# The recurrence's side work on GpSimd's queue, in four steps a group instead of three

## The chip, the cores and the metric

The kernel runs on one core of one Trainium2 chip. The metric is the device time of one execution in microseconds (us). The engines are PE (TensorE, matmuls), DVE (VectorE), ACT (ScalarE), POOL (GpSimd) and SP (SyncE); the last issues most DMAs. ACT and POOL can issue DMAs too; all of them move over the core's 16 DMA engines.

## The reference, cut to what matters

Two models run one after the other on 256 tokens of width 1024, with 256 context tokens beside them in the first. The first has two layers, each a token mixer followed by a mixture of 32 experts, of which each token uses two:

```python
def expert_block(args):               # xb: a block of gathered tokens, e: its expert
    xb, e = args
    hb = jax.nn.silu(xb @ w1[e]) * (xb @ w3[e])
    return hb @ w2[e]
...
y = ypad.reshape(-1, D)[dest] * weights[order][:, None]
return jnp.zeros_like(xt).at[tok].add(y)
```

The second model is a layer of dilated attention and then a diagonal complex recurrence:

```python
A = lax.complex(a_re, a_im);  dt = jnp.exp(log_dt)[:, None]
a_bar = jnp.exp(A * dt)
b_bar = ((a_bar - 1.0) / A)[..., None] * Bm          # Bm = b_re + i b_im
bu = jnp.einsum('bsgc,gpc->bsgp', uf, b_bar)
_, states = lax.associative_scan(combine, (a_elems, bu), axis=1)
y = jnp.einsum('bsgp,gcp->bsgc', states, Cm).real    # Cm = c_re + i c_im
```

The parameters of the recurrence (a, b, c, dt) do not depend on the tokens, so that tables of powers and products of them can be made long before the recurrence runs.

## The kernel before

`run()` calls the stages in order: setup, `phase_a`, `moe(0)`, `phase_b`, `moe(1)`, `phase_c` (attention), `phase_d` (recurrence). The change lies in `moe(1)`, the second mixture. Its 32 experts are worked through in ten groups, p = 0 to 9, by the list `PLAN[1]`: two experts in p = 0 and 1, three in p = 2 to 5, four in p = 6 to 9. The instructions of the groups stand in the order in which the code is written (`tc.manual_schedule()`), on every engine.

An expert's weights come as six DMAs of 1 MB on SP's queue (`w()`, L176), so a group has 12, 18 or 24 of them. They land in eleven slots of 1 MB, seven named `wt` and four named `wu`, that are used in turn: a load takes the slot of the load eleven before it, and waits until PE has read that one. The DMAs of SP and ACT share eight semaphores in turn, so that an SP load also waits until the DMA eight before it, whoever issued it, has landed.

A group runs so: `hidden()` multiplies the gathered tokens with w1 and w3 in four blocks, (h,m) = (0,0), (0,1), (1,0), (1,1); each block reads a sixth of the group's loads. Between the matmuls of the first two blocks the group before is scattered back, four times: PE makes `px` (L1322, L1323), DVE multiplies it with the gate into `yt` (L1325), POOL adds that to `x` (L1329). `px` has two buffers, so the third `px` waits for the first `yt`. Then come the gate product `sg` (ACT L1284, DVE L1285 and L1286), the gathering of the next group's tokens (PE L1233), transposes (L1292, L1259), and `result()`, which multiplies with w2 into `py` (PE L1304) and ends with the two `yl` on DVE (L1312). At the start of a group DVE also makes the one-hot matrices of the next one (L1214 to L1222).

The tables of the recurrence are made beside this by a generator, `ssm_side()`, whose `yield`s cut it into steps. `next(side, None)` runs one step where it stands: in `hidden()` after the blocks (0,0) and (0,1), and after `result()`, from p = 1 on. The steps are, by number: 1 the DMAs of parameters and raw tensors; 2 PE transposes of a (L1854) and powers on DVE; 3 `turned(0)`, 32 PE transposes of the raw b (L1846) and copies by ACT and DVE; 4 arithmetic on DVE; 5 `turned(1)`, the same transposes for c; 6 arithmetic; 7 nothing; 8 the power tables E and U (DVE); 9 `bb` and `EB` (DVE and POOL); 10 `Bg` (DVE and POOL); 11 sixteen PE transposes of `Bg` (L2031) and a store of 1 MB to the scratch `Sd`; 12 `Wd`; 13 four matmuls (L2047) and `KC` on DVE; 14 to 17 the same as 10 to 13 for the other half; 18 to 20 `CP` and the first powers (`turn`); 21 to 24 further powers (`unit`), then two stores of 1 MB. With three steps a group, p = 1 runs steps 1 to 3, p = 2 steps 4 to 6, and so on to p = 8.

Of the kernel before, what the change touches and what calls it, by code (L numbers as in the profile page):

```python
# [11 lines left out]
F32 = mybir.dt.float32  # L12
# [9 lines left out]
P = 128  # L22
# [96 lines left out]
class Model:  # L119
# [911 lines left out]
    def moe(self, l):  # L1031
        nc, A, tc, m = self.nc, self.A, self.tc, self.m
# [51 lines left out]
        def rest():  # L1084

            nonlocal side, G2
            m.c4.close()
            xl = c3.enter_context(tc.tile_pool(name=f"xl{l}", bufs=1, side="right"))
            G2 = G2 or gates(xl)
            if l == 1:  # L1090
                self.row_bc(A["final_g"], m.fg, nc.sync)
                side = self.ssm_side(xl, psum)

        fixed, by_count = PLAN[l]
# [171 lines left out]
        def hidden(ws, xT, between=iter(()), turn=True, ts=PAIR):  # L1266
            ph = [psum.tile([P, 512], F32, name=f"ph{m}") for m in range(2)]
            for h in range(2):
                for m in range(2):
                    for k in range(4 * h, 4 * h + 4):  # L1270
                        for j, r in slots(ts)[1]:
                            nc.tensor.matmul(ph[m][r, :], lhsT=xT[:, k, r], rhs=ws[m, j, h][:, k % 4, :],  # L1272
                                             start=(k == 0), stop=(k == NK - 1))
                        if k % 2 == 1:
                            next(between, None)
                    if h == 0 and turn:
                        next(side, None)
            for _ in between:
                pass

            sg = xe.tile([P, 512], F32, name="sg", tag="sg")
            sv = sg.rearrange("p (h k c) -> p h k c", h=2, k=2)
            pv = [v.rearrange("p (h c k) -> p h k c", h=2, k=2) for v in ph]
            nc.scalar.activation(sv, pv[0], AF.Sigmoid)  # L1284
            nc.vector.tensor_mul(sv, sv, pv[0])  # L1285
            nc.vector.tensor_mul(sv, sv, pv[1])  # L1286
            return sg
# [519 lines left out]
    def ssm_side(self, p, psum):  # L1807


        nc, A = self.nc, self.A  # L1810
        ident = self.ident
# [11 lines left out]
        ad = x2[0:64, 0:256].rearrange("p (i d q) -> p i d q", i=2, d=2)  # L1823
        for i, n in enumerate(("ssm_a_re_2", "ssm_a_im_2")):
            for d in range(2):
                nc.scalar.dma_start(ad[:, i, d, :], A[n][0])
        s = p.tile([P, 16, 64], F32, name="sv", tag="sc")
        dt = s[:, 14]
        a = A["ssm_log_dt_2"]
        nc.scalar.dma_start(dt, bass.AP(tensor=a.tensor, offset=a.offset, ap=[[0, P], [1, 64]]))  # L1830

        bb = p.tile([P, 2, 64, 16], F32, name="bb")
        cc = p.tile([P, 2, 64, 16], F32, name="cc")
        b12 = p.tile([P, 2, 64, 16], F32, name="b12", tag="big")
        raws = [self.w(A[n][0].rearrange("g q c -> g (q c)"), (1024,), rows=64) for n in ("ssm_b_re_2", "ssm_b_im_2")]
        raws += [self.w(A[n][0].rearrange("g c q -> g (c q)"), (1024,), rows=64) for n in ("ssm_c_re_2", "ssm_c_im_2")]

        def turned(half):
            for i in (2 * half, 2 * half + 1):
                dst = (b12 if i < 2 else cc)[:, i % 2]  # L1840
                rv = raws[i].rearrange("g (q c) -> g c q", c=16) if i < 2 else \
                    raws[i].rearrange("g (c q) -> g c q", c=16)
                for c8 in range(2):
                    pt = pst()
                    for c in range(8):
                        nc.tensor.transpose(pt[0:64, c * 64:(c + 1) * 64], rv[:, c8 * 8 + c, :], ident[:64, :64])  # L1846
                    for h in range(2):
                        self.copy(dst[64 * h:64 * h + 64, :, c8 * 8:c8 * 8 + 8],
                                  pt[0:64].rearrange("p (c g) -> p g c", c=8), "av"[h])

        yield
        pt = pst()
# [42 lines left out]
        er, th, n, r, r2, cr = (s[:, i] for i in range(6))  # L1895
# [79 lines left out]
        for h in range(2):  # L1975
            rows = slice(64 * h, 64 * h + 64)
# [14 lines left out]
            return xt().rearrange("p (g c) -> p g c", c=16)  # L1991

        yield

        for hf in range(2):
            fr, fi = (F[:, i, 32 * hf:32 * hf + 32] for i in range(2))
# [8 lines left out]
        stage = self.cx.rearrange("p b d -> p (b d)")  # L2005
# [5 lines left out]
            ts(EB[64:128, sel, :, i], E[64:128, 0:4, bot], sb_, None, op0=ALU.mult)  # L2011

        bbM = p.tile([P, 32, 16], F32, name="bbM")
        for hf in range(2):
            yield

            Bg = p.tile([P, 16, 4, 2, 16], F32, name="Bg", tag="big")
            for sidx in range(4):
                j = 3 - sidx
                xa = ga()  # L2020
                gt(xa, hv(bb[:, 0], hf), gb(EB[:, 0, j, 0, 32 * hf:32 * hf + 32]), op=ALU.mult)
                tt(xb, hv(bb[:, 1], hf), gb(EB[:, 0, j, 1, 32 * hf:32 * hf + 32]), op=ALU.mult)
                xs = [t.rearrange("p (a b) c -> p a b c", b=2) for t in (xa, xb)]
                tt(Bg[:, :, sidx], xs[0], xs[1], op=ALU.add)
                if j == 0:
                    gt(bbM, xa, xb, op=ALU.add)
            yield
            for q in range(4):
                pt = pst()
                for i in range(4):  # L2030
                    nc.tensor.transpose(pt[:, i * P:(i + 1) * P], Bg[:, 4 * q + i].rearrange("p s g c -> p (s g c)"),  # L2031
                                        ident)
                self.copy(stage[:, q * 512:(q + 1) * 512], pt)
            nc.scalar.dma_start(self.Sd[hf], stage)
            yield

            Wd = p.tile([P, 4, 32, 16], F32, name="Wd", tag="big")
            for j in range(4):
                xa = ga()
                gt(xa, hv(c1, hf), gb(EB[:, 1, j, 0, 32 * hf:32 * hf + 32]), op=ALU.mult)  # L2040
                tt(xb, hv(cim, hf), gb(EB[:, 1, j, 1, 32 * hf:32 * hf + 32]), op=ALU.mult)
                tt(Wd[:, j], xa, xb, op=ALU.add)
            yield
            KC = p.tile([P, 4, 64], F32, name="KC")
            for ch in range(4):
                pt = pst()
                nc.tensor.matmul(pt, lhsT=bbM[:, 8 * ch:8 * ch + 8, :].rearrange("p g c -> p (g c)"),  # L2047
                                 rhs=Wd[:, :, 8 * ch:8 * ch + 8, :], start=True, stop=True)
                kt = xt().rearrange("p (d n) -> p d n", d=4)
                tt(kt, pt.rearrange("p (d n) -> p d n", d=4), self.cc("bmask")[:, None, :].to_broadcast([P, 4, P]),  # L2050
                   op=ALU.mult)
                nc.vector.tensor_reduce(KC[:, ch].rearrange("p (d c) -> p d c", d=4), kt.rearrange("p d (g c) -> p d c g", c=16), axis=AX.X,
                                        op=ALU.add)
            nc.scalar.dma_start(self.Sm[:, 1280 + 256 * hf:1536 + 256 * hf], KC.rearrange("p k n -> p (k n)"))
        yield

        CP = p.tile([P, 2, 32, 16], F32, name="CP", tag="sc")
        for h in range(2):
            rows = slice(64 * h, 64 * h + 64)
            nc.gpsimd.tensor_copy(CP[rows], cc[rows].rearrange("p i (a g) c -> p i a g c", g=2)[:, :, :, h, :])  # L2060
        for c0, t in ((0, CP.rearrange("p i a c -> p (i a c)")), (1024, E1.rearrange("p t i a -> p (t i a)")),
                      (1792, U1[:, 2])):
            nc.scalar.dma_start(self.Sm[:, c0:c0 + t.shape[1]], t)


        T = [t.rearrange("p i g c -> p (i g c)").rearrange("p (a k) -> p a k", k=64) for t in (bb, cc)]
# [22 lines left out]
        def unit(c):  # L2089
            v = [t[:, :, c:c + 16] for t in T]  # L2090
            a_, b_ = two()
            gt(a_, v[0], v[0], op=ALU.mult)
            tt(b_, v[1], v[1], op=ALU.mult)
            tt(b_, a_, b_, op=ALU.add)
            ts(b_, b_, -0.5, 1.5, op0=ALU.mult, op1=ALU.add)
            for t in v:
                tt(t, t, b_, op=ALU.mult)
# [11 lines left out]
        for c in range(0, 64, 16):  # L2109
            yield  # L2110
            unit(c)
        for n, t in enumerate(T):
            nc.scalar.dma_start(self.Sd[2 + n], t.rearrange("p a k -> p (a k)"))

    def phase_d(self):
        nc, A, tc = self.nc, self.A, self.tc
# [70 lines left out]
        E1 = SM[:, 1024:1280].rearrange("p (t i a) -> p i a t", i=2, a=32)  # L2187
        KC = SM[:, 1280:1792].rearrange("p (k d c) -> p k d c", k=8, c=16)
        for half in range(2):
# [17 lines left out]
        def blocks(h):  # L2207

            for g in range(8):
                nc.scalar.activation(Kd[h].rearrange("p (k d g c) -> p (k d) g c", k=4, d=4, g=8)[:, :, g, :],  # L2210
                                     KC[:, 4 * h:4 * h + 4].rearrange("p k d c -> p (k d) c"), AF.Copy,
                                     scale=self.cc("bmask")[:, 16 * g:16 * g + 1])
# [148 lines left out]
```

## Time and profile before

| | |
|---|---|
| time, median of 3 runs | 2028.18 us (2027.03 to 2028.48) |
| profiled execution, its own time | 2020.63 us |
| its span, first to last instruction | 2018.8 us, mean granted TensorE clock 0.945 |
| busy share of the span | PE 86%, DVE 54%, ACT 29%, POOL 29% |
| second mixture's groups p = 2 to p = 9 | from 1075.34 us to about 1499 us of the span |

The rows below come from the profiled execution; its time is 7.55 us, 0.37%, under the median of the runs. Times in rows are us from the start of the span. "idle before <-releaser" says how long an engine stood still before the row and what ended that.

### The profile page before, as it was taken

To read this page: it belongs to the slowest core of one execution; us is meant where nothing else is said; L and a number is where in the kernel's file an instruction comes from. 1 tells how busy PE (TensorE), PEld (TensorE's weight loads), DVE (VectorE), ACT (ScalarE), POOL (GpSimd) and SP (SyncE) were. 2 spreads that over 40 slices of the span, in tenths; PEclk is the share of its full clock that TensorE was granted. 3 is DMA by queue.
4 is the path that set the end of the run, shared out by engine and by line. 5 is a ranking of instruction groups with operands and counts; after the bars stand their busy time and mean duration, and the time that the engine had idled before them with its cause. 6 is when DMAs were issued, how large, how long until landed. Compare 5 with 4: busy or idle time off the path is not lost. (4 is left out here: it accounts for less than half of the span.)

```text
span 2018.8 us, 29905 instructions
## 1 busy us (share of the span) xinstructions
PE 1745.1 (86%) x11305; PEld 1047.0 (52%) x11305; DVE 1091.3 (54%) x2184; ACT 592.2 (29%) x1041; POOL 589.1 (29%) x467
## 2 busy tenths in 40 slices
PE   6999879999999968999698778767759999998878
PEld 3746743333334326886533222221219899886877
DVE  3576663333333336655654656463226677776875
ACT  3254320100101015443411000000015556554654
POOL 1211323233232324222301132232004343451552
PEclk9999989999999988999898988898889999998989
DMA  9487469999999955855779999999996454445041
GB/s 352 159 320 255 162 274 384 419 419 420 420 419 420 421 230 178 260 183 182 288 267 406 424 397 421 425 424 425 425 360 212 160 170 136 141 163 200 1 160 40
DMA packets 177860, 581.71 MB, mean 288 GB/s; under 512 B 28600, under 2 KB 97676, under 8 KB 127472
## 3 DMA queue, kind: packets, MB, share of 16 engines
q1 hardware_dynamic: 160208, 561.49, 71.5%
q10 hardware_dynamic: 15440, 11.10, 1.8%
q0 software_dynamic: 2064, 7.15, 1.1%
q8 instruction: 91, 1.49, 0.3%
q14 instruction: 57, 0.47, 0.1%
HBM read 572.38 MB, written 12.37 MB: 290 GB/s over the span
## 5 line engine op out<-in xcount | busy, mean ns | idle before, releaser
L1272 PE MATMUL ph<-wu,xT 128*32 128x512 f32 (+1 forms) x1744 | 365.0, 616 | 23.1 <-DMA wu<-in_moe_w_dram 23.1
L1329 POOL TENSOR_TENSOR x<-x,yt 128x512 f32<-128x512 f32 x88 | 113.9, 1298 | 568.8 <-DVE yt L1325 568.7
L210 DVE TENSOR_TENSOR wl<-wt,wh 128x1024 fp32r<-128x1024 f32 x121 | 192.5, 1609 | 60.1 <-ACT wh L207 50.8
L1272 PE MATMUL ph<-wt,xT 128*32 128x512 f32 (+1 forms) x712 | 188.6, 655 | 40.6 <-DMA wt<-in_moe_w_dram 40.6
L1325 DVE TENSOR_TENSOR yt<-px,G 128x512 f32<-128x512 f32 x144 | 98.5, 689 | 200.6 <-PE px L1323 197.7
L492 PE MATMUL mm<-hh,wh 128*128 128x256 f32 (+1 forms) x704 | 192.8, 300 | 4.5 <-ACT hh L463 2.6
L492 PE MATMUL mm<-hh,wl 128*128 128x256 f32 (+1 forms) x704 | 190.0, 296 | 0.0
L492 PE MATMUL mm<-hl,wh 128*128 128x256 f32 (+1 forms) x704 | 189.1, 294 | 0.0
L207 ACT ACTIVATE wh<-wt 128x1024 fp32r<-128x1024 f32 x162 | 163.8, 1049 | 75.9 <-PE mm L492 35.1
L1304 PE MATMUL py<-wu,hTe 128*32 128x512 f32 (+1 forms) x888 | 176.2, 623 | 10.0 <-DMA wu<-in_moe_w_dram 5.5
L1272 PEld LDWEIGHTS ph<-wu,xT 128*32 128x32 f32 (+1 forms) x1744 | 79.9, 116 | 180.2 <-issue 129.8
L210 POOL TENSOR_TENSOR wl<-wt,wh 128x1024 fp32r<-128x1024 f32 x41 | 106.5, 2597 | 127.4 <-ACT wh L207 103.5
L492 PEld LDWEIGHTS mm<-hh,wh 128*128 128x128 f32 x704 | 131.7, 195 | 11.0 <-ACT hh L463 4.3
L1312 DVE SCALAR_TENSOR_TENSOR yl<-py,sv,yh 128x512 fp32r<-128x512 f32 x46 | 34.5, 751 | 189.7 <-ACT yh L1311 189.7
L492 PEld LDWEIGHTS mm<-hh,wl 128*128 128x128 f32 x704 | 131.7, 194 | 3.8 <-issue 1.2
L492 PEld LDWEIGHTS mm<-hl,wh 128*128 128x128 f32 x704 | 131.1, 192 | 3.3 <-DVE hl L464 0.3
L1284 ACT ACTIVATE sg<-ph 128x512 f32<-128x512 f32 x23 | 13.7, 597 | 381.7 <-PE ph L1272 381.7
L1272 PEld LDWEIGHTS ph<-wt,xT 128*32 128x32 f32 (+1 forms) x712 | 39.1, 118 | 126.5 <-DMA wt<-in_moe_w_dram 71.1
L1304 PEld LDWEIGHTS py<-wu,hTe 128*32 128x32 f32 (+1 forms) x888 | 47.1, 120 | 90.6 <-issue 70.2
L1304 PE MATMUL py<-wt,hTe 128*32 128x512 f32 (+1 forms) x360 | 85.0, 637 | 7.8 <-DMA wt<-in_moe_w_dram 7.8
L1322 PEld LDWEIGHTS px<-yh,OT 128*128 128x128 f32 x144 | 27.5, 191 | 123.2 <-issue 99.7
L1311 ACT ACTIVATE yh<-py,sv 128x512 fp32r<-128x512 f32 x46 | 31.6, 687 | 195.0 <-PE py L1304 195.0
(614 smaller groups left out, 3436.3 us busy)
## 6 DMA issues: line engine op xcount, KB each, us to landing
wu<-in_moe_w_dram SPq DMA_DIRECT2D x259, 1024.0 KB
wt<-in_moe_w_dram SPq DMA_DIRECT2D x120, 1024.0 KB
wt<-in_ada_w_dram SPq DMA_DIRECT2D x40, 1024.0 KB
wt<-in_attn_w_in_dram SPq DMA_DIRECT2D x80, 512.0 KB
wt<-in_odd_w_in_dram SPq DMA_DIRECT2D x12, 1024.0 KB
wu<-in_ada_w_dram SPq DMA_DIRECT2D x8, 1024.0 KB
wt<-in_ssm_w_in_dram SPq DMA_DIRECT2D x6, 1024.0 KB
wt<-in_even_w_in_dram SPq DMA_DIRECT2D x5, 1024.0 KB
```

Source lines behind the costliest of these rows:

```text
L207: nc.scalar.activation(hi, v, AF.Copy)
L210: (nc.gpsimd if self.part % 4 == 3 else nc.vector).tensor_tensor(lo, v, hi.bitcast(F32), op=ALU.subtract)
L492: r = self.nc.tensor.matmul(out, lhsT=lhs[k][a], rhs=rhs[k][b], start=(start and i == 0), stop=(stop and i == 3 * n - 1))
L1272: nc.tensor.matmul(ph[m][r, :], lhsT=xT[:, k, r], rhs=ws[m, j, h][:, k % 4, :], start=(k == 0), stop=(k == NK - 1))
L1284: nc.scalar.activation(sv, pv[0], AF.Sigmoid)
L1304: nc.tensor.matmul(py[n][r, :], lhsT=hT[:, k, r], rhs=ws[2, j, k // 2][:, k % 2, n * 512:(n + 1) * 512], start=(k == 0), stop=(k == 3))
L1311: nc.scalar.activation(yh[:, c], py[n], AF.Copy, scale=sv[:, 1:2])
L1312: nc.vector.scalar_tensor_tensor(yl[:, c], py[n], sv[:, 1:2], yh[:, c].bitcast(F32), op0=ALU.mult, op1=ALU.subtract)
L1322: nc.tensor.matmul(pc, lhsT=OT[:, i, :], rhs=yh[:, c], start=True, stop=False)
L1325: nc.vector.tensor_mul(t, pc, G2[:, i // 2, c])
L1329: nc.gpsimd.tensor_tensor(xs[i][:, c], xs[i][:, c], t, op=ALU.add)
```

## The change

Six things are done at once.
1. The row broadcast of `final_g` (`fg`, 512 KB) goes from SP's to POOL's queue.
2. The five DMAs of parameters (a_re, a_im, log_dt) and all stores to the scratch tensors `Sd` and `Sm` go from ACT's to POOL's queue, which has semaphores of its own.
3. The four raw tensors (256 KB each) no longer take slots of the weights; they go by POOL's queue into a tile `raw`, in the space where the table `bb` lies later.
4. `hidden()` runs a step of the generator after three blocks, (0,0), (0,1) and (1,0), instead of two; with the one after `result()` that makes four a group.
5. The first store to `Sd` of each half is issued a step later, the two of `KC` together at the end of their loop, with a second buffer for `KC`.
6. The last two stores stand in a step of their own.

So p = 1 now runs steps 1 to 4, p = 2 steps 5 to 8, p = 3 steps 9 to 12, p = 4 steps 13 to 16, p = 5 steps 17 to 20, p = 6 steps 21 to 24 and p = 7 the last stores.

```diff
-                self.row_bc(A["final_g"], m.fg, nc.sync)
+                self.row_bc(A["final_g"], m.fg, nc.gpsimd)
...
-                    if h == 0 and turn:
+                    if h + m < 2 and turn:
                         next(side, None)
...
-                nc.scalar.dma_start(ad[:, i, d, :], A[n][0])
+                nc.gpsimd.dma_start(ad[:, i, d, :], A[n][0])
...
-        bb = p.tile([P, 2, 64, 16], F32, name="bb")
...
-        raws = [self.w(A[n][0].rearrange("g q c -> g (q c)"), (1024,), rows=64) for n in ("ssm_b_re_2", "ssm_b_im_2")]
-        raws += [self.w(A[n][0].rearrange("g c q -> g (c q)"), (1024,), rows=64) for n in ("ssm_c_re_2", "ssm_c_im_2")]
+        raw = p.tile([P, 2, 1024], F32, name="raw", tag="bb")
+        raws = [raw[0:64, i] for i in range(2)] + [raw[64:P, i] for i in range(2)]
+        for r, n in zip(raws, ("ssm_b_re_2", "ssm_b_im_2", "ssm_c_re_2", "ssm_c_im_2")):
+            nc.gpsimd.dma_start(r, A[n][0].rearrange("g a b -> g (a b)"))
...
-            nc.scalar.dma_start(self.Sd[hf], stage)
             yield
+            nc.gpsimd.dma_start(self.Sd[hf], stage)
...
-            KC = p.tile([P, 4, 64], F32, name="KC")
+            KC = p.tile([P, 4, 64], F32, name="KC", bufs=2)
...
+        yield
         for n, t in enumerate(T):
-            nc.scalar.dma_start(self.Sd[2 + n], t.rearrange("p a k -> p (a k)"))
+            nc.gpsimd.dma_start(self.Sd[2 + n], t.rearrange("p a k -> p (a k)"))
```

Three places show what moves. First POOL's own order in p = 1 after the change, from the first two additions of the scatter on (`x_8570` is the tile that takes a_re and a_im):

```order
L1329 TENSOR_TENSOR x<-x,yt 128x512 x2
L1826 DMA x_8570<-in_ssm_a_re_dram 64x64 x2
L1826 DMA x_8570<-in_ssm_a_im_dram 64x64 x2
L1830 DMA sv<-in_ssm_log_dt_dram 128x64
L1838 DMA raw<-in_ssm_b_re_dram 64x1024
L1838 DMA raw<-in_ssm_b_im_dram 64x1024
L1838 DMA raw<-in_ssm_c_re_dram 64x1024
L1838 DMA raw<-in_ssm_c_im_dram 64x1024
L1329 TENSOR_TENSOR x<-x,yt 128x512 x8
```

The nine DMAs stand behind the first two additions of p = 1; before, the parameters stood on ACT's queue and the raw tensors on SP's, and POOL had twelve additions in a row here.

Second, PE in p = 2, where `turned(1)` transposes the raw c. Before it stood behind the fourth `px`, at the end of block (0,1):

```order
L1322 MATMUL px_8906<-yh,OT 128x512
L1323 MATMUL px_8906<-yl,OT 128x512
L1846 MATMUL tr<-C,wt 64x64 x32
L1272 MATMUL ph_8828<-wu,xT 32x512 x2
L1272 MATMUL ph_8828<-wt,xT 32x512
```

After the change it stands behind the second `px`, at the end of block (0,0):

```order
L1322 MATMUL px_8874<-yh,OT 128x512
L1323 MATMUL px_8874<-yl,OT 128x512
L1849 MATMUL tr<-C,raw 64x64 x32
L1272 MATMUL ph_8851<-wt,xT 32x512 x2
L1272 MATMUL ph_8851<-wu,xT 32x512
```

In the same way the transposes of the raw b (before: behind `py` of p = 1) now stand between the blocks (1,0) and (1,1) of p = 1.

Third, DVE from the end of p = 2 through p = 3 after the change (`U` is the last of step 8, `bb` and `EB` are step 9, `Bg` is step 10, `cx` takes the transposes of step 11):

```order
L1982 COPY U_9143<-sv 64x32 x3
...
L1222 TENSOR_TENSOR OH<-C,rkt 128x2x32 x2
L1325 TENSOR_TENSOR yt<-px_9232,G_8021 128x512
L1325 TENSOR_TENSOR yt<-px_9246,G_8021 128x512
L2003 TENSOR_TENSOR x_8570<-b_8578,F 128x512
...
L1325 TENSOR_TENSOR yt<-px_9287,G_8021 128x512
L1325 TENSOR_TENSOR yt<-px_9301,G_8021 128x512
L2027 TENSOR_TENSOR x_8570<-bb,EB 128x512
...
L225 COPY cx<-tr 128x512 x2
L1285 TENSOR_TENSOR sg<-sg,ph_9222 128x512
```

Before, step 8 stood ahead of the gate product of p = 3, step 9 behind `py` of p = 3, and step 10 in block (0,1) of p = 4; now steps 8 to 10 follow each other on DVE with only the one-hots and the `yt` of p = 3 between them. On PE the sixteen transposes of `Bg` (step 11, now L2036) stand between the blocks (1,0) and (1,1) of p = 3:

```order
L1272 MATMUL ph_9222<-wt,xT 32x512 x3
L1272 MATMUL ph_9222<-wu,xT 32x512
L2036 MATMUL tr<-C,Bg 128x128 x16
L1272 MATMUL ph_9223<-wt,xT 32x512 x3
L1272 MATMUL ph_9223<-wu,xT 32x512
```

Before, they stood between the blocks (0,1) and (1,0) of p = 4.

## Rows read from the trace of the kernel before

**Rows 1.** The page's first line.

```profile
span 2018.8 us, 29905 instructions
```

**Rows 2.** Windows: us; busy of PE, PEld, DVE, ACT, POOL; clock; DMA share; GB/s.

```profile
1070.00:1120.00 50.00, 43.54 (x328) 16.75 (x324) 25.25 (x76) 9.08 (x16) 5.06 (x4) 0.90 1.01 426
...
1192.00:1198.00 6.00, 4.60 (x30) 2.70 (x22) 2.81 (x9) 0.97 (x3) 0.00 (x0) 1.00 0.53 178
...
1300.00:1500.00 200.00, 142.52 (x718) 37.62 (x718) 65.92 (x140) 12.14 (x21) 34.84 (x30) 0.89 1.01 422
```

**Rows 3.** SP's queue, waits from 1000 to 1520: total us, times, longest.

```profile
SPq L176 <- DMA Sd<-cx: 33.4, 2, 19.2
SPq L176 <- DMA Sm<-KC: 22.5, 2, 11.4
```

**Rows 4.** SP's timeline: start, us, the DMA issued.

```profile
1068.08 0.33 SPq L176 DMA_DIRECT2D wu<-in_moe_w_dram  x1
...
1175.51 0.33 SPq L176 DMA_DIRECT2D wt<-in_moe_w_dram  x1
1195.20 0.33 SPq L176 DMA_DIRECT2D wu<-in_moe_w_dram  x1
```

**Rows 5.** PE's timeline, single rows from p = 1 to p = 9.

```profile
1051.78 0.24 PE L1854 MATMUL tr<-C,x 64*128 64x64 f32 x1 [0.26 <-DMA x<-in_ssm_a_im_dram]
...
1071.42 1.12 PE L1846 MATMUL tr<-C,wt 64*64 64x64 f32 x16
...
1075.34 1.07 PE L1272 MATMUL ph<-wu,xT 128*32 128x512 f32 x2
...
1081.65 0.62 PE L1272 MATMUL ph<-wu,xT 128*32 128x512 f32 x2
...
1086.69 1.08 PE L1846 MATMUL tr<-C,wt 64*64 64x64 f32 x16
1091.50 1.84 PE L1846 MATMUL tr<-C,wt 64*64 64x64 f32 x16 [3.73 <-DVE cc L225]
...
1102.82 0.50 PE L1233 MATMUL px<-OTh,OH 128*128 128x512 f32 x1
...
1115.14 0.60 PE L1272 MATMUL ph<-wt,xT 128*32 128x512 f32 x2
...
1181.53 3.84 PE L2031 MATMUL tr<-C,Bg 128*128 128x128 f32 x16 [8.38 <-DVE Bg L2024]
...
1495.87 0.62 PE L1304 MATMUL py<-wt,hTe 128*32 128x512 f32 x2 [1.49 <-DMA wt<-in_moe_w_dram]
```

**Rows 6.** POOL: two additions, a DMA's issue; DMAs with KB and us to landing.

```profile
1045.96 2.50 POOL L1329 TENSOR_TENSOR x<-x,yt 128x512 f32<-128x512 f32 x2 [39.19 <-DVE yt L1325]
...
969.26 0.57 POOL L383 DMA_DIRECT2D G<-ADd  x1
...
th<-Gr POOLq DMA_DIRECT2D x16, 128.0 KB, 2.6
G<-ADd POOLq DMA_DIRECT2D x3, 512.0 KB, 8.5
```

**Rows 7.** Windows of steps 4, 8, 9, 10, 12 and 13, then one of PE alone.

```profile
1082.44:1089.44 7.00, 5.33 (x48) 2.06 (x40) 6.25 (x27) 1.07 (x2) 1.29 (x1) 1.00 1.01 428
1130.96:1144.16 13.20, 10.50 (x71) 3.99 (x68) 12.26 (x54) 1.20 (x2) 3.36 (x3) 1.00 1.01 425
1158.19:1167.89 9.70, 8.29 (x40) 1.73 (x39) 9.07 (x18) 0.00 (x0) 3.12 (x2) 0.82 1.01 422
1170.36:1181.30 10.94, 2.79 (x20) 0.71 (x18) 8.33 (x9) 0.00 (x0) 8.28 (x7) 0.80 1.01 425
1207.55:1214.92 7.37, 5.68 (x31) 1.51 (x32) 6.85 (x9) 0.00 (x0) 3.13 (x2) 1.00 1.02 429
1218.58:1225.27 6.69, 5.43 (x20) 1.18 (x20) 6.55 (x9) 0.00 (x0) 2.06 (x2) 0.74 1.01 421
1093.00:1097.00 4.00, 4.00 (x24) 1.09 (x25) 1.37 (x2) 0.70 (x2) 0.00 (x0) 0.50 1.01 422
```

More of the change, by code (lines that the diff above doesn't have):

```diff
@@ L1829, in ssm_side @@
         a = A["ssm_log_dt_2"]
-        nc.scalar.dma_start(dt, bass.AP(tensor=a.tensor, offset=a.offset, ap=[[0, P], [1, 64]]))
-        bb = p.tile([P, 2, 64, 16], F32, name="bb")
+        nc.gpsimd.dma_start(dt, bass.AP(tensor=a.tensor, offset=a.offset, ap=[[0, P], [1, 64]]))
         cc = p.tile([P, 2, 64, 16], F32, name="cc")
         b12 = p.tile([P, 2, 64, 16], F32, name="b12", tag="big")
-        raws = [self.w(A[n][0].rearrange("g q c -> g (q c)"), (1024,), rows=64) for n in ("ssm_b_re_2", "ssm_b_im_2")]
-        raws += [self.w(A[n][0].rearrange("g c q -> g (c q)"), (1024,), rows=64) for n in ("ssm_c_re_2", "ssm_c_im_2")]
+        raw = p.tile([P, 2, 1024], F32, name="raw", tag="bb")
+        raws = [raw[0:64, i] for i in range(2)] + [raw[64:P, i] for i in range(2)]
+        for r, n in zip(raws, ("ssm_b_re_2", "ssm_b_im_2", "ssm_c_re_2", "ssm_c_im_2")):
+            nc.gpsimd.dma_start(r, A[n][0].rearrange("g a b -> g (a b)"))
         def turned(half):
+            g = slice(64 * half, 64 * half + 64)
             for i in (2 * half, 2 * half + 1):
@@ L1845, in turned @@
                     for c in range(8):
-                        nc.tensor.transpose(pt[0:64, c * 64:(c + 1) * 64], rv[:, c8 * 8 + c, :], ident[:64, :64])
+                        nc.tensor.transpose(pt[0:64, c * 64:(c + 1) * 64], rv[:, c8 * 8 + c, :], ident[g, g])
                     for h in range(2):
@@ L1993, in ssm_side @@
         yield
+        bb = p.tile([P, 2, 64, 16], F32, name="bb", tag="bb")
         for hf in range(2):
@@ L2013, in ssm_side @@
         bbM = p.tile([P, 32, 16], F32, name="bbM")
+        KCs = []
         for hf in range(2):
@@ L2053, in ssm_side @@
                                         op=ALU.add)
-            nc.scalar.dma_start(self.Sm[:, 1280 + 256 * hf:1536 + 256 * hf], KC.rearrange("p k n -> p (k n)"))
+            KCs.append(KC)
         yield
+        for hf, KC in enumerate(KCs):
+            nc.gpsimd.dma_start(self.Sm[:, 1280 + 256 * hf:1536 + 256 * hf], KC.rearrange("p k n -> p (k n)"))
         CP = p.tile([P, 2, 32, 16], F32, name="CP", tag="sc")
@@ L2062, in ssm_side @@
                       (1792, U1[:, 2])):
-            nc.scalar.dma_start(self.Sm[:, c0:c0 + t.shape[1]], t)
+            nc.gpsimd.dma_start(self.Sm[:, c0:c0 + t.shape[1]], t)
         T = [t.rearrange("p i g c -> p (i g c)").rearrange("p (a k) -> p a k", k=64) for t in (bb, cc)]
```

## The prediction

> **What bounds the kernel now.** I read the page's first line, then windows over the second mixture, then the waits of SP's queue, then the timelines of SP, PE, DVE and POOL in p = 1 to 5. The profiled execution takes 2020.63 us, of which 2018.8 are its span [rows 1]; all sums are made against it and carried over to the median, 7.55 us higher. A change within 0.2% (4 us) can't be told from none.
>
> In the second mixture the DMA engines move 422 to 426 GB/s, with a share of 1.01 [rows 2]: one load of 1 MB takes 1.0486 / 424 = 2.47 us. So 18 loads of a group take 44.5 us and 24 take 59.4, while PE needs about 40 for p = 2 with its transposes (1075.34 to 1115.14) [rows 5]. The stretch is bound by the stream of weights. It can be rebuilt: the fourth load of p = 2 is issued at 1068.08 [rows 4], when the first half of `py` of p = 1 frees its slot; PE gets the last at 1495.87 [rows 5]. Of these 427.8 us, 165 loads take 407.6, about 4.9 MB of stores 12.1, the one visible hole (178 GB/s from 1192 to 1198 [rows 2], 6 x (1 - 178/424)) 3.5, and start and landing the other 4.6.
>
> Two things stop this stream: SP standing at a semaphore, and PE, since a load needs the slot that PE read eleven loads (27 us) earlier. A short stall of PE costs nothing: it waited 8.38 for `Bg` at 1181.53 [rows 5] and the DMA rate held until the hole, for which SP's wait for the `Sd` store is enough: SP issues nothing from 1175.51 to 1195.20 [rows 4].
>
> **What is removed.** Four slots no longer go to raw tensors. Of the loads of p = 2, those that wait for the first half of `py` of p = 1 were the fourth and fifth; now they are the eighth and ninth. The stream is four loads further on at that point: -9.9 us. SP's waits for DMAs of ACT's queue end: 33.4 for `Sd` and 22.5 for `KC` alone [rows 3]. But the rate shows only the 3.5 us hole, so that is all I count: -3.5. Together -13.4.
>
> The Trainium skill has a rule on this (page "DMA: Bandwidth & Descriptors", section "Issuing engines are not separate DMA queues"): all issuing engines share the 16 DMA engines, and another one saves only the time to issue. By it the 3.5 would be nothing and the sum 3.5 higher. The trace differs, since SP stood 19.2 us behind one store [rows 3]: here the queue's order of waits is saved, not issue time.
>
> **What is added in p = 1.** The parameters now stand on POOL behind two additions that end at 1045.96 + 2.50 = 1048.46 [rows 6]; before, PE waited 0.26 for a_im at 1051.78 [rows 5]. Four issues of 0.57 [rows 6] put the last a_im at 1050.7. Its landing, 16 KB, is bounded by 2.6 us (128 KB) and 8.5 (512 KB) [rows 6]; I take 4.5, nearer the smaller size but with other DMAs in flight. So PE waits until about 1055, 4 us more (bounds 2 and 8).
>
> The Trainium skill prices this path (same page, section "Anatomy of one DMA — SWDGE (gpsimd) path") at 2.0 us plus bytes / 436e3, an estimate of 2.0 us here, which would make the sum 2.5 lower; it fits the 128 KB row and not the 512 KB one.
>
> The transposes of the raw b, 1071.42 to 1075.34 [rows 5], move ahead of `py`: 3.9 us by which the slots of `py` come later. The raw tensors are issued by about 1054 and needed at about 1059, so I let them cost nothing (bounds 0 and 2, the same landing rows). Sum: +8, bounds 6 and 12.
>
> **What moves: the tables.** This is where I expect the time to go. I count from S, the start of p = 2. The load of p = 2 numbered n waits for the block that reads n - 11.
>
> p = 2. Loads 8 and 9 start at about S - 2.3 (half of `py` is 3.5 us, and issue to start 1.2), so the stream would finish load 14 at S + 15.0. Load 15 needs block (0,1). Before, that block ended at S + 11.3 (1086.69), ahead of `turned(1)` [rows 5]. Now `turned(1)` comes first, and its third and fourth part wait for DVE: `yl` until 1.6, step 4 7.0 [rows 7], one-hots and two `yt` 2.5 (1167.89 to 1170.36, between two windows of [rows 7]), copies 2.5: S + 13.6. Then (0,1) takes 5.0 (1081.65 to 1086.69) plus up to 2.5, because PE's granted clock after such a wait was 0.50 (1.2 of 2.4 GHz) from 1093 to 1097 [rows 7]. Load 15 starts near S + 22: a hole of 7. Group p = 2 as a whole stays at about 40.6.
>
> p = 3. DVE now has in order: `yl` 1.6, step 8 13.2, one-hots and two `yt` 2.5, step 9 9.7, two `yt` 1.3, step 10 10.9 [rows 7]: 39.2 us after the start of p = 3. PE stands before the transposes of `Bg`, having only three blocks to do (some 15 us): it waits about 25 us in all, partly at the third `px`, where it needs the first `yt`, the rest at the transposes. These take 3.8 [rows 5], block (1,1) 4: its slots come free at 47, and load 39 starts at 48.2 after the start of p = 3, or S + 88.8. Without a hole the stream would have finished load 38 at 15.0 + 24 x 2.47 = S + 74.3. So the holes of p = 2 and 3 together are 14.5 us. The end of the group takes the usual 12.3 (1102.82 to 1115.14 [rows 5]): p = 3 lasts 59.3 us against 44.5 of loads.
>
> p = 4. `yl` 1.6, step 12 7.4, one-hots and `yt` 2.5, step 13 6.7 [rows 7], two `yt` that wait for PE's slowed block (3.4), step 14 10.9 like step 10: 32.5; transposes 3.8, block (1,1) 4: slots free at 40.3, the next load at S + 141.4. Eighteen loads and one store from S + 88.8 end at S + 135.8: a hole of 5.6. p = 4 lasts 52.6.
>
> p = 5. Step 16 and 17 like 12 and 13 hold block (0,1) until about 21.5 after its start, S + 174.0 + 1.2; twelve loads and one store after S + 141.4 end at S + 173.5: a hole of 1.7. From p = 6 the loads take 59.4 a group, and what is left on DVE hides under them, as powers of the same kind do in p = 7 and 8 before (422 GB/s from 1300 to 1500 [rows 2]).
>
> Holes: 14.5 + 5.6 + 1.7 = 21.8, say +22. Bounds: step 8 loses 2.6 if it runs without POOL's additions beside it, and block (1,1) runs at full clock, some 4 in p = 3, 3 in p = 4, 1.7 in p = 5: 13. On the other side POOL's products start later behind the additions in steps 9, 10 and 14, 2 to 3 each: 31.
>
> Nothing for the rest: POOL's 19 issues of 0.57 are 11 us on an engine busy 35 of 200 us [rows 2]; `fg` moved early leaves SP with less; the second `KC` buffer and the shared space of `bb` add no instruction. If POOL's additions are delayed by the DMAs in front of them, the next to wait is the `yt` of p = 2, some 20 us later.
>
> **Sum:** -13.4 + 8 + 22 = +16.6 us, bounds +6 and +30. From 2020.63 that is 2037.2, from the median 2044.8; I say 2044, own range 2034 to 2056.
>
> **Rivals.** (a) *Faster: the eleven slots cover the stalls.* If the holes stay under 1.4 us, -13.4 + 8 wins: 2022.8 without holes. For it: PE's 8.4 us stall cost nothing. Against: the stall of p = 3 is three times that, and the waits are counted in DVE's order, which a faster queue doesn't shorten. It decides where PE's stall in p = 3 exceeds what the stream is ahead. Chance 0.15.
> (b) *No change: gains and holes cancel*, with the steps of p = 3 and 4 cheaper than their windows, holes of 2 to 9: 2028. For it: several windows hold waits that may vanish (12.26 busy of 13.20, 8.33 of 10.94 [rows 7]). Against: that gives back 4 to 5 us a group at most. Chance 0.12.
> (c) *The queues gain nothing:* POOL's own semaphores make SP or POOL wait as ACT's did, the hole of 3.5 stays, the rest goes as forecast: 3.5 more, 2048, inside the forecast's range. Chance 0.10. The rule of the Trainium skill on issuing engines (above) would come to the same; the trace's 19.2 us behind one store speaks against it.
>
> **Chances and range.** The forecast has 0.63, (c) 0.10, (a) 0.15, (b) 0.12. So slower 0.73, same 0.12, faster 0.15. The range runs from 2022, where most of (a) and (b) are taken in, to 2056; I leave 0.07 below it and 0.08 above.
>
> **What would show it.** Right: no wait of SP on `Sd` or `KC`; the fourth to ninth loads of p = 2 issued before the second half of `py`; a_im's wait on PE of 2 to 8 us in p = 1; PE idle some 25 us in p = 3, ended by `yt` and `Bg`; the DMA rate falling below 424 there and in p = 4; p = 6 starting some 200 us after p = 2; the last weight at about 1512 on PE. Wrong: a rate that stays at 424 through p = 3, or DVE finishing `Bg` less than 30 us into p = 3.

## The result and the profile after

The change makes the kernel slower: 2052.13 us, median of 4 runs (2048.79 to 2054.54), against 2027.82 for the kernel before beside it; the ratio is 1.0116, 95% interval 1.0104 to 1.0128. That is +24.3 us where +16 was forecast. The page's first line after:

```profile
span 2048.7 us, 29909 instructions
```

The spans differ by 29.9 us [rows 1], but 5.9 of these were there before p = 1 began (its first matmul stands at 1041.16 before and 1047.08 after; POOL's `G` DMA, ahead of everything that was changed, was already 5.8 late). From the first `ph` of p = 1 to the first `px` behind the last `py` of the mixture the trace has 24.5 us more, and that is the part to explain: p = 1 is 6.6 us longer, p = 2 to 5 are 25.6 longer and p = 6 to 9 are 7.7 shorter. p = 6 alone takes 50.0 us, less than the 59.4 of its 24 loads, so it uses loads that landed while PE stood still.

PE's timeline after, rows that waited in p = 1 to p = 5 (some are left out):

```profile
1060.37 0.33 PE L1857 MATMUL tr<-C,x 64*128 64x64 f32 x1 [3.15 <-DMA x<-in_ssm_a_im_dram]
1062.60 0.37 PE L1857 MATMUL tr<-C,x 64*128 64x64 f32 x1 [1.90 <-DMA x<-in_ssm_a_im_dram]
1070.75 1.11 PE L1849 MATMUL tr<-C,raw 64*64 64x64 f32 x16 [1.17 <-DMA raw<-in_ssm_b_im_dram]
...
1099.64 1.91 PE L1849 MATMUL tr<-C,raw 64*64 64x64 f32 x16 [5.70 <-DVE cc L225]
...
1142.45 0.79 PE L1322 MATMUL px<-yh,OT 128*128 128x512 f32 x1 [4.72 <-DVE yt L1325]
1168.59 3.84 PE L2036 MATMUL tr<-C,Bg 128*128 128x128 f32 x16 [17.94 <-DVE Bg L2029]
...
1220.49 3.72 PE L2036 MATMUL tr<-C,Bg 128*128 128x128 f32 x16 [7.60 <-DVE Bg L2029]
...
1283.21 1.11 PE L1292 MATMUL tr<-C,sg 128*128 128x128 f32 x4 [11.30 <-DVE sg L1286]
```

Read it downwards: in p = 1 PE waits for parameters and raw tensors, 6.2 us in all, where it had waited 0.26 [rows 5]; in p = 3 it stands 4.7 us at the third `px` and 17.9 in front of the transposes of `Bg`; in p = 4 and p = 5 it waits again for DVE. None of these waits is for a weight.

Windows after, where the stream of weights stops (columns as in [rows 2]):

```profile
1103.00:1111.00 8.00, 8.00 (x60) 2.15 (x56) 3.40 (x7) 0.00 (x0) 2.56 (x2) 0.91 0.37 118
1128.00:1160.00 32.00, 16.61 (x108) 4.50 (x101) 25.98 (x85) 0.69 (x1) 11.07 (x9) 0.88 1.01 426
1167.00:1175.00 8.00, 6.41 (x40) 3.80 (x44) 3.32 (x5) 1.68 (x3) 3.05 (x3) 0.64 0.21 85
1225.00:1233.00 8.00, 6.53 (x50) 3.66 (x42) 3.34 (x10) 1.47 (x3) 2.69 (x3) 1.00 0.83 306
1259.00:1265.00 6.00, 6.00 (x52) 1.82 (x48) 1.87 (x4) 0.00 (x0) 2.67 (x3) 1.00 0.60 217
1287.00:1294.00 7.00, 7.00 (x61) 1.97 (x64) 0.69 (x1) 0.66 (x1) 0.00 (x0) 0.87 0.49 167
1300.00:1500.00 200.00, 140.58 (x736) 38.59 (x730) 54.05 (x123) 11.32 (x20) 32.35 (x26) 0.91 1.01 425
```

The second row is the instructive one: from 1128 to 1160 PE is busy for half of the time and the rate is still 426 GB/s. The stream runs on until the eleven slots are full; the hole comes behind the stall, from 1167 to 1175, when PE is at work again. SP's timeline after shows it from the other side: after the second load of p = 4 it issues nothing for 23 us.

```profile
1152.81 0.33 SPq L176 DMA_DIRECT2D wu<-in_moe_w_dram  x1
1176.21 0.91 SPq L176 DMA_DIRECT2D wt<-in_moe_w_dram  x2
```

From p = 6 on the rate is 425 and nothing is lost. Summed over windows of 2 us, with 424 GB/s as full, the holes from the start of p = 2 (1087.83) to 1300 come to about 27 us.

SP's waits after, from 1000 to 1540 (columns as in [rows 3]):

```profile
SPq L176 <- PE ph L1272: 220.1, 41, 22.9
SPq L176 <- PE py L1304: 99.7, 24, 19.9
SPq L176 <- DMA wt<-in_moe_w_dram: 43.9, 27, 2.7
```

The waits for `Sd` and `KC` of [rows 3] are gone, and PE has taken their place: SP now waits for slots.

### The profile page after: what moved, and what is told of

It reads as the page before. It is cut to its first block, busy times and chain, and to the rows that moved or that the text cites. A ratio compares the mean times of both kernels' runs of the same rounds, so it can differ in the third digit from the quotient of the medians.

```text
span 2048.7 us, 29909 instructions
## 1 busy us (share of the span) xinstructions
PE 1738.9 (85%) x11305; PEld 1049.6 (51%) x11305; DVE 1084.8 (53%) x2184; ACT 592.1 (29%) x1041; POOL 597.6 (29%) x486
## 5 line engine op out<-in xcount | busy, mean ns | idle before, releaser
L210 DVE TENSOR_TENSOR wl<-wt,wh 128x1024 fp32r<-128x1024 f32 x121 | 191.3, 1599 | 60.3 <-ACT wh L207 53.6
L1272 PE MATMUL ph<-wt,xT 128*32 128x512 f32 (+1 forms) x720 | 175.5, 647 | 28.7 <-DMA wt<-in_moe_w_dram 28.7
```

Of the source, the lines that this page charges most:

```text
L210: (nc.gpsimd if self.part % 4 == 3 else nc.vector).tensor_tensor(lo, v, hi.bitcast(F32), op=ALU.subtract)
```

## The experiments

Eleven kernels ran. The runs of a kernel spread over some 0.3 to 0.7%, so two measures stand side by side: the ratio to the kernel before on the same chip, and, from each profile, the time from the first `ph` of p = 1 to the first `px` behind the last `py` of p = 9, which leaves out what varies before and behind the mixture. There is one profile of each kernel; p = 0, which only e10 and e11 change, lasts 26.1 us in all but e10. All times are us; the columns p = 1 to 5 are the lengths of these groups, from one first `ph` to the next.

| kernel | median | ratio, 95% interval | p=1 | p=2 | p=3 | p=4 | p=5 | p=1 to end |
|---|---|---|---|---|---|---|---|---|
| before | 2027.4 to 2028.6 | 1 | 34.2 | 39.8 | 40.6 | 49.8 | 51.2 | 458.3 |
| changed | 2052.13 | 1.0116 (1.0104 to 1.0128) | 40.8 | 40.3 | 60.3 | 51.6 | 54.7 | 482.8 |
| e1 | 2032.19 | 1.0017 (1.0001 to 1.0032) | 40.0 | 37.3 | 44.8 | 48.4 | 50.7 | 460.9 |
| e2 | 2055.46 | 1.0141 (1.0119 to 1.0162) | 40.0 | 40.5 | 60.4 | 51.8 | 53.6 | 485.8 |
| e3 | 2026.75 | 0.9991 (0.9978 to 1.0004) | 33.5 | 37.0 | 43.6 | 49.3 | 50.8 | 453.5 |
| e4 | 2025.94 | 0.9991 (0.9978 to 1.0003) | 33.9 | 38.2 | 43.5 | 49.2 | 50.8 | 456.1 |
| e5 | 2047.77 | 1.0096 (1.0075 to 1.0118) | 39.9 | 40.5 | 60.5 | 51.7 | 54.8 | 482.4 |
| e6 | 2042.42 | 1.0073 (1.0054 to 1.0092) | 42.3 | 40.5 | 56.8 | 50.6 | 51.5 | 475.3 |
| e7 | 2052.51 | 1.0121 (1.0106 to 1.0136) | 40.4 | 40.5 | 60.4 | 51.7 | 54.6 | 482.9 |
| e8 | 2021.04 | 0.9962 (0.9948 to 0.9977) | 33.4 | 39.0 | 44.8 | 48.4 | 50.7 | 455.6 |
| e9 | 2024.07 | 0.9978 (0.9968 to 0.9988) | 33.8 | 36.8 | 44.6 | 48.3 | 50.6 | 453.2 |
| e10 | 2025.88 | 0.9988 (0.9978 to 0.9999) | 33.4 | 37.3 | 42.9 | 47.7 | 50.1 | 450.7 |
| e11 | 2025.38 | 0.9982 (0.9971 to 0.9992) | 33.4 | 38.6 | 44.9 | 48.3 | 50.6 | 455.2 |

**The change taken apart.** e1 is the changed kernel with the old number of steps:

```diff
-                    if h + m < 2 and turn:
+                    if h == 0 and turn:
```

> The changed kernel with three steps of the table generator a group again; queues and the tile for the raw tensors as in the change. Theory (the loss is the density of the steps on DVE): no new holes in the stream of weights in p = 2 to 5; what stays is the gain of 13.4 us and about 6 us of PE waiting in p = 1 for the parameters on POOL's queue (5.1 us measured after the change, and a slow clock behind it): 2027.8 - 13.4 + 6 = 2020 us. Rival (the loss is what POOL's queue does: late landings, its own waits): the time stays above 2040 us.

Measured: ratio 1.0017. The rival is out: the queues are not the loss. But the gain that was expected beside it did not come either; p = 1 is 5.8 us longer than before, and the rest only 3.2 shorter.

e2 is the reverse, the kernel before with only that line changed to `h + m < 2`:

> The kernel before with four steps a group and nothing else. Theory: p = 2 starts as before (1075.3 us of the span, since the transposes of the raw b only move inside p = 1), and p = 2 to 5 then last as long as after the change, 207 us: 6 to 7 us faster than the changed kernel, 2045 us, or up to 3.5 us more where SP's waits for stores add to it. Rival (POOL's queue): about 2028 us or less.

Measured: 1.0141, more than the changed kernel, and 2055 us where 2045 to 2048.5 was expected. p = 3 lasts 60.4 us and p = 5 53.6, as there, so the loss is the fourth step, whichever queue carries the DMAs. I had p = 1 as before; it is 5.8 longer, since the transposes of the raw b now come before the raw b has landed (PE waits 2.8 us for it). And SP still waits for stores, the third row here:

```profile
SPq L176 <- PE ph L1272: 115.6, 35, 15.1
...
SPq L176 <- DMA Sd<-cx: 40.6, 2, 24.3
```

e3 is e1 with the parameters issued by ACT again (`nc.scalar` in place of `nc.gpsimd` for a_re, a_im and log_dt):

> As the first run, with the five parameter DMAs on ACT's queue again. Theory: PE's wait in p = 1 goes too, the gain of 9.9 (four slots) and 3.5 (the hole at the Sd store) stands alone: 2027.8 - 13.4 = 2014 to 2015 us. Rival (four loads more in flight gain nothing, since something else bounds the start): 2020 us or more.

Measured: 0.9991, an interval that holds 1. p = 1 is back at 33.5 us, so the parameters' wait is 6 to 7 us of p = 1 (e1 against e3). But of the 13.4 us only 1.6 appear in the medians and 4.7 in the trace. That is the largest miss of these runs.

e4 moves only `fg` and the stores to POOL; parameters and raw tensors stay where they were, three steps:

> The kernel before with only fg and the stores to Sd and Sm on POOL's queue (the stores where the change puts them); three steps, parameters on ACT, raw tensors in the ring. Theory: the hole of 3.5 us at 1192 is gone and SP waits for no store: 2024 us. Rival (another issuing engine saves only issue time): 2027 to 2028 us.

Measured: 0.9991, 2.1 us less in the trace. This lies between the two theories, and a difference of this size can't be told from none; that the hole at 1192 is gone is seen in its rate, which stays at 397 or above in every window of 2 us from 1086 to 1300.

**Why the four slots bring so little.** The rate over the whole of p = 1 tells what the freed slots can have taken (the kernel before, the changed one, e4, e3 and e9, which follows below):

```profile
1041.16:1075.34 34.18, 31.18 (x162) 13.06 (x158) 17.03 (x51) 5.67 (x10) 5.04 (x4) 0.99 0.99 346
1047.08:1087.83 40.75, 33.07 (x163) 13.20 (x159) 16.53 (x51) 5.47 (x10) 9.65 (x13) 0.92 0.98 340
1050.38:1084.32 33.94, 31.09 (x162) 12.97 (x158) 16.93 (x51) 5.67 (x10) 5.05 (x4) 0.99 0.94 319
1051.07:1084.60 33.53, 30.79 (x163) 12.80 (x159) 16.82 (x50) 5.58 (x10) 7.14 (x8) 1.00 1.00 346
1049.64:1083.47 33.83, 30.83 (x162) 12.80 (x158) 16.83 (x50) 5.58 (x10) 7.20 (x8) 1.00 1.01 405
```

e3 has the four slots that e4 lacks. It moves 346 GB/s against 319 for 33.5 us, 0.9 MB more, which is one load and not four: 2.1 us at 424 GB/s, near the 2.6 by which the traces of e3 and e4 differ.

In e3 the rate is low for 16 us of p = 1, just when the freed slots should fill. Windows of e3:

```profile
1058.00:1062.00 4.00, 4.00 (x18) 1.50 (x18) 1.37 (x3) 0.00 (x0) 3.76 (x6) 1.00 0.90 277
1062.00:1066.00 4.00, 4.00 (x22) 1.40 (x20) 3.62 (x15) 0.60 (x1) 1.27 (x1) 1.00 0.99 266
1066.00:1070.00 4.00, 4.00 (x20) 1.83 (x17) 2.93 (x10) 0.21 (x1) 0.00 (x0) 1.00 1.05 275
1070.00:1074.00 4.00, 2.54 (x18) 1.79 (x17) 2.12 (x8) 1.26 (x3) 0.00 (x0) 1.00 1.01 293
```

The share is about 1 and the rate 266 to 293: the engines are occupied, but with something slow. The kernel before has such a stretch too, so the change did not bring it:

```profile
1054.00:1058.00 4.00, 4.00 (x20) 1.29 (x18) 3.52 (x18) 0.60 (x1) 0.00 (x0) 1.00 1.04 257
1058.00:1062.00 4.00, 3.72 (x20) 2.31 (x16) 2.09 (x5) 0.60 (x1) 0.00 (x0) 1.00 1.04 224
```

The raw tensors lie on 64 partitions and take long to land in the changed kernel too, as the tile `raw` of that kernel shows (minimum, median, maximum over the four):

```profile
DMA to landing us min/median/max: 10.7/14.6/16.2
```

e8 leaves them out of e3 (`nc.gpsimd.memset(raw, 0.0)` in place of the four DMAs):

> The kernel of e3 (three steps, parameters on ACT) with the four raw tensors left out: their tile is filled with zeros by POOL, so the tables and the output are not the reference's. Theory (the four freed slots bring little because the raw tensors' own transfers, 10 to 16 us from issue to landing, hold the DMA rate at 234 to 304 GB/s for 16 us just when the slots are free): 6 us less than e3, 2021 us. Rival (slots or PE hold the start of p = 2 anyway): as e3, 2026 to 2027 us.

e9 keeps their bytes and spreads each over 128 partitions:

```diff
-            nc.gpsimd.dma_start(r, A[n][0].rearrange("g a b -> g (a b)"))
+            nc.gpsimd.dma_start(raw[:, k // 2, 512 * (k % 2):512 * (k % 2) + 512],
+                                A[n][0].rearrange("g a b -> g (a b)").rearrange("g (h x) -> (g h) x", h=2))
```

> The kernel of e3 with the same four raw tensors, the same bytes on the same queue, but each spread over 128 partitions in rows of 2 KB instead of 64 in rows of 4 KB; their values land in other places, so the tables and the output are not the reference's. Theory (transfers to 64 partitions move at half the rate, and hold up the weights beside them): 4 to 6 us less than e3, 2021 to 2023 us, and no stretch under 350 GB/s in p = 1. Rival (POOL's queue or the raw tensors' bytes themselves cost it): as e3, 2026 to 2027 us.

Measured: e8 0.9962, e9 0.9978. The same windows of e9:

```profile
1058.00:1062.00 4.00, 3.75 (x18) 1.34 (x16) 2.15 (x4) 0.00 (x0) 3.66 (x5) 1.00 0.98 290
1062.00:1066.00 4.00, 4.00 (x20) 1.29 (x18) 3.46 (x18) 0.60 (x1) 0.00 (x0) 1.00 1.03 413
1066.00:1070.00 4.00, 4.00 (x22) 2.45 (x18) 2.08 (x6) 0.60 (x1) 0.00 (x0) 1.00 1.02 426
1070.00:1074.00 4.00, 2.53 (x16) 1.32 (x16) 2.41 (x9) 0.87 (x2) 0.00 (x0) 1.00 1.01 426
```

The same bytes on the same queue: 413 to 426 GB/s in the last three windows as soon as 128 partitions are used, and they land after 7.4 to 11.4 us where e3 has 9.9 to 16.2. So 12 of the 16 us are the raw tensors' layout. The first window is low in both kernels, so that one is something else. The edit also halves the rows, from 4 KB to 2 KB, and no run separates this from the partitions.

What the layout costs in time is less clear. The medians put e8 6 us and e9 3 us under e3; in the traces e8 is 2.1 us longer than e3 and e9 0.4 shorter. By its rate over p = 1, e9 is 6.9 us of stream ahead of e4, but only 3.0 shorter in the trace. In e8 the reason is to be seen, as the stream is far enough ahead to run into the slots in p = 2 (SP waits 23.4 us for `ph` there):

```profile
1086.00:1090.00 4.00, 4.00 (x34) 0.97 (x26) 2.14 (x4) 0.00 (x0) 2.09 (x2) 1.00 0.76 260
1103.00:1107.00 4.00, 4.00 (x44) 1.20 (x40) 0.69 (x1) 0.60 (x1) 0.00 (x0) 1.00 0.59 178
```

e10 issues the parameters (by ACT) and raw tensors in p = 0:

```diff
-                    if p == 1:
+                    if p == (0 if l == 1 else 1):
                         rest()
+                        if l == 1:
+                            next(side)
```

and one more `yield` behind the first step.

> The kernel of e3 with the space for the tables opened, and the parameters and raw tensors issued, in p = 0 instead of p = 1, with an empty step added so that all later steps stand where they stood. In p = 0 the DMA rate falls to 32 GB/s for 10 us (window 1030 to 1040 of before), so theory has the raw tensors cost nothing there: 6 us less than e3, about 2021 us, as without them. Rival (the transfers are dear wherever they stand, or the early issue waits for the early weight slots that share the space): 2026 us or more.

Measured: 0.9988. In p = 0 the raw tensors land in 3.7 to 5.7 us. One window of e10 there:

```profile
1040.00:1044.00 4.00, 0.52 (x4) 0.38 (x2) 0.48 (x1) 2.37 (x3) 0.78 (x2) 1.00 1.03 229
```

The rate is 229 GB/s at a full share. From p = 1 to the end this is the shortest kernel, 7.6 us under the one before. But p = 0 lasts 32.6 us instead of 26.1, so that 1.1 is left of it. PE is busy for 0.52 of these 4 us: ACT's five issues of the parameters (1038.40 to 1041.57) stand ahead of the gate's activation in p = 0, as PE's waits from 1030 to 1060 show (what waits, for what, us in total, times, longest):

```profile
PE tr L1292 <- DVE sg L1286: 4.5, 1, 4.5
```

e11 is e10 with the parameters on POOL:

> As e10 (space, parameters and raw tensors in p = 0, three steps a group), but with the parameters on POOL's queue as in the change, since in e10 ACT's five issues waited for the early weight slots and made the gate product of p = 0 late (PE waited 4.5 us for it), while from p = 1 to the end of the mixture e10 took 7.6 us less than the kernel before. Theory: both stand together, 7 to 8 us under the kernel before, 2020 us. Rival (what p = 1 gains is given back in p = 2 and 3, whatever p = 0 does): 2025 us or more.

Measured: 0.9982 (0.9971 to 0.9992). The wait in p = 0 is gone, but p = 1 to the end is 455.2, only 3.1 less than before: the rival, for the most part. Of the kernels that compute everything it has the lowest ratio, about 4 us under the kernel before, but the intervals of e3, e4 and e10 overlap its own.

**The density of the steps.** e6 puts an empty step ahead of the first transposes of `Bg` in the changed kernel, so that they stand behind `py` of p = 3:

```diff
             yield
+            if hf == 0:
+                yield
             for q in range(4):
```

> The changed kernel with one empty step ahead of the first transposes of Bg, so that they stand behind py of p = 3 and no longer between its blocks (1,0) and (1,1). Theory (DVE's order sets the length: the gate product of p = 3 stands behind Bg on DVE): p = 3 lasts 55 us instead of 60, 2047 us. Rival (PE's standing in front of the transposes, 17.9 us, is the loss): p = 3 lasts 45 us or less, 2036 us or less.

Measured: 1.0073. PE's wait in front of `Bg` is gone from p = 3, but p = 3 still lasts 56.8 us, near the 55 of the theory. The timeline of e6 in p = 3 shows where the wait went:

```profile
1143.18 0.79 PE L1322 MATMUL px<-yh,OT 128*128 128x512 f32 x1 [4.61 <-DVE yt L1325]
1157.77 0.50 PE L1233 MATMUL px<-OTh,OH 128*128 128x512 f32 x1 [2.70 <-DVE yt L1325]
1170.69 1.12 PE L1292 MATMUL tr<-C,sg 128*128 128x128 f32 x4 [10.67 <-DVE sg L1286]
```

What PE no longer waits for at the transposes it waits for at `yt` and `sg`, which stand behind the same table steps on DVE. The rest of e6's gain comes mostly from p = 4 and 5, whose steps moved too.

e5 is the changed kernel with the parameters on ACT, as in e3, but with four steps:

> The changed kernel with the five parameter DMAs on ACT's queue again, four steps a group. Theory: PE's waits for a_im in p = 1 (5.1 us) and the slow clock behind them go, p = 1 lasts 6 to 7 us less and nothing gives it back: 2045 to 2047 us. Rival (the holes of p = 2 and 3 grow by what p = 1 loses): 2050 to 2052 us.

Measured: 1.0096, an interval that overlaps the changed kernel's, and 0.3 us less in the trace. There the wait for a_im fell to 0.3 us, and the transposes of the raw b wait instead:

```profile
PE tr L1849 <- DMA raw<-in_ssm_b_re_dram: 2.8, 1, 2.8
PE tr L1849 <- DMA raw<-in_ssm_b_im_dram: 1.3, 1, 1.3
```

p = 1 is 39.9 us instead of 40.8. Whoever comes first hides the other; the medians' 4 us stay unexplained by the trace.

e7 puts POOL's copies into `CP` ahead of the stores of `KC`:

> The changed kernel with the two copies into CP on POOL ahead of the two stores of KC instead of behind them. In p = 5 of the changed kernel DVE stands 3.5 us before it may overwrite cc, which POOL's copies read. Theory (the copies are late because they stand behind DMAs on POOL): p = 5 lasts 2 to 3.5 us less than 54.7, the time is 2049 us. Rival (the copies themselves are the wait): no difference, 2052 us.

Measured: 1.0121, no difference. DVE's wait fell from 3.47 to 2.34 us, and its next one, for POOL's first product, rose from 1.22 to 1.98. POOL's timeline of e7 shows the queue in front of it, two additions, two copies and five issues, 1263.05 to 1271.70:

```profile
1263.05 1.28 POOL L1329 TENSOR_TENSOR x<-x,yt 128x512 f32<-128x512 f32 x1 [6.28 <-DVE yt L1325]
1265.57 1.28 POOL L1329 TENSOR_TENSOR x<-x,yt 128x512 f32<-128x512 f32 x1 [1.24 <-DVE yt L1325]
1266.79 2.16 POOL L2064 COPY CP<-cc 64x1024 f32<-64x1024 f32 x2
1268.90 1.12 POOL L2066 DMA_DIRECT2D Sm<-KC  x2
...
1271.70 0.25 POOL L2091 TENSOR_TENSOR x<-bb 128x32 f32<-128x32 f32 x1
```

## Why the prediction was right, and where it was off

**The direction and its mechanism were right.** The loss is DVE's order in p = 3. `Bg` was forecast 39.2 us after the start of p = 3 and ends at 1168.44, 40.3 after it. That this is so close is in part luck: step 8 took 10.4 us where 13.2 stood in the sum (without POOL's additions beside it, as the lower bound had it), and step 9 took 13.4 where 9.7 stood, since POOL had made its first products ahead of it before, and now DVE waits for one, which stands behind POOL's additions, as the upper bound had it:

```profile
1146.48 1.53 DVE L2004 TENSOR_TENSOR bb<-x,x 128x512 f32<-128x512 f32 x1 [2.18 <-POOL x L2002]
```

p = 2, 3 and 4 were forecast at 40.6, 59.3 and 52.6 us and last 40.3, 60.3 and 51.6. Load 39, for which SP stands still in p = 3, was forecast 88.8 us after the start of p = 2, at 1176.6, and is issued at 1176.21. The place of the holes was right too: behind (0,1) of p = 2, 5.8 us (8 x (1 - 118/424)) where 7 was forecast, and behind the stall of p = 3. e2 shows that the fourth step does it alone, e6 that it is DVE's order and not the place of the transposes on PE. Rival (a), that eleven slots cover the stall, failed as the second and third window rows show: PE stops at 1137.7, and 30 us later the rate falls. Rival (b) failed with it. Rival (c), that the queues gain nothing, is not far off for the single parts (e3, e4), though SP's waits for stores did go.

**The sum by its own terms.** p = 1 to the start of p = 2, +8: here 40.75 against 34.18 less the 3.92 of the moved transposes, +10.5, inside the bounds 6 and 12. The a_im waits were 5.1 instead of 4 (the rows of the forecast give 3.5), and the raw b, which I let cost nothing, 1.2; its price of up to 2 was in the bounds. That was luck too: the raw tensors land after 10.7 to 16.2 us, where I had bounded them by 8.5, and PE stood at the parameters meanwhile; in e5, without that wait, the raw b costs 4.1. The holes, +22: 27, inside 13 and 31. With the -13.4 this gives 24.1 where 24.5 is measured, but the -13.4 is not what the runs show, as told below.

**The step that was mis-sized** is p = 5, forecast with a hole of 1.7 and, by the 200 us from p = 2 to p = 6, at 47 us. It lasts 54.7, and its holes (1259 to 1265 and 1287 to 1294) are 2.9 + 4.2 = 7.1 us. I followed only block (0,1) there. Steps 18 and 19 hold DVE from 1263.50 to 1281.68, and the gate product stands behind them: PE waits 11.3 us for `sg`, and the slots of `py` come free late. It is the same mechanism as in p = 3, further on than I followed it.

**A term that stood for the wrong reason** is the -9.9 for four slots. Taken alone (e3 against e4) it is worth 2.6 us in the trace and nothing by the medians. I counted when the slots are free, not when the loads can have landed: in e3 the DMA moved one load more in p = 1, not four. And where the stream does get ahead (e8), the slots stop it in p = 2. Nor do the four slots bring 9.9 beside the four steps. e2 has the four steps without the slots, with nearly the same p = 1 (40.0 us) and the same holes (27 us). By the sum it would lie 9 us above the changed kernel; it lies 3.1 above it in the trace and some 5 by the ratios. So the other terms are not lost in full. One reason can be read in the changed kernel: the stream goes on while p = 1 grows, 340 GB/s over 40.75 us against 346 over 34.18 before, 2.0 MB or 4.8 us more. That the sum comes to 24.1 is in this part luck, errors of opposite sign.

By edits, along the chain of kernels e4, e3, e1, changed, the traces give -2.1 (stores and `fg`), -2.6 (raw tensors out of the ring), +7.3 (parameters on POOL) and +21.9 (fourth step): 24.5. The terms of such a sum are not independent; in another order they would be others.

**What stays open.** How much the 64-partition transfers cost in time: medians (6 us) and traces (none) of e8 disagree. The profiled execution of e8 is 4.1 us shorter than that of e3, but it gains 2.9 ahead of p = 1 and 3.3 behind the mixture, where the two kernels do not differ, and loses 2.1 between. And the traces of e10 and e11 differ by 4.5 us from p = 1 on, where the same work runs: the holes up to 1300 come to about 4 us in e10 and 8 in e11, but why the slots stop e11 longer is not shown.

## What to carry to other kernels

Side work that is cut into steps between the steps of a main loop has to fit each engine's time in that group, in order: add up what stands on the in-order engine ahead of the next thing that the main loop needs, over neighbouring groups, and compare it with how far the buffered transfers can run ahead. A slot that is freed earlier is worth only what the DMA can move into it by then, and what follows must be able to use it. When several terms of a forecast share one resource, test the edits one by one: here a gain of 9.9 us, worth 2.6 alone, and losses that were counted in full hid each other in a sum that came out right.

## What was not expected of the hardware

Four transfers of 256 KB to 64 partitions, beside loads of 1 MB to 128 partitions, held the rate of all to 266 to 293 GB/s with a share of about 1 (e3, 1062 to 1074), and landed after 9.9 to 16.2 us; with only the parameters' small transfers beside them they moved at 229 GB/s (e10). The same bytes over 128 partitions left 413 to 426 (e9). The Trainium skill bears on this (page "SBUF — State Buffer", section "Door 1: The DMA port swizzle"): partitions 0 to 63 reach only half of the ports, for which it measured 196 GB/s in a transfer of 1 MB. The 229 of e10 is above that; there two of the four tensors lie on partitions 0 to 63 and two on 64 to 127. What such a transfer takes from others beside it, that section does not say, and these windows show it.
